# Two layers of a hybrid decoder trunk: moving DMA steps, the write of x and half of the token sums

## Chip, cores and metric

One core of a Trainium2 chip runs the kernel. The metric is device time in microseconds (us), the median of the runs. TensorE (PE) multiplies, VectorE (DVE) and ScalarE (ACT) work on vectors, GpSimd (POOL) on small operations; ACT, POOL and SyncE (SP) issue DMAs, each in the order of its own queue.

## The reference

The kernel computes two decoder layers over 512 tokens of width 1024, all in float32. Each layer adds three things to x:

```
h = rmsnorm(x); x += (gated sum of convolution, sparse attention, latent attention) @ w_out
x += cross_attention(rmsnorm(x), rmsnorm(mem))
gate, up = split(rmsnorm(x) @ w_gate_up);  x += (silu(gate) * up) @ w_down      # hidden width 2816
```

After the second layer comes one more rmsnorm.

## The kernel before

**Products.** A float32 product is made of three matmuls: each operand is cast to a high part (ACT, line 92) and a low part is the difference (DVE, line 93), and high x high, high x low and low x high are summed. Weights go through `raw` (two buffers of 1 MB, loaded by SP, line 101), then `wh` and `wl` (three buffers each). Lines 85 to 87 are one such triple of matmuls (`mm3`); lines 1261 to 1263 are the triple of the last residual.

**Fewer products.** The gate-up product and the down product use a scheme with seven products in place of eight of a 2 x 2 block product, which needs sums and differences of blocks on both sides.
- Weight sums: `summed(l)` lists 152 DMAs ("steps") that copy and add blocks of `w_gate_up` and `w_down` into the DRAM tensors `up` and `down`. They are issued by POOL (line 372, `tick`): every triple of matmuls adds `paced["rate"]` to an account, and when it reaches 1 the next step is issued, tied by a semaphore to that triple. The rate is 0.17 in the mixer and up to the feed-forward part, 0.07 in it. Steps of layer 1 are listed before layer 0's last residual, and there the rate is 0.06. All steps of a layer must be issued before its last residual.
- Token sums: lines 1488 to 1504 make four sums `t` of the normed, transposed x for each half `kk` of the rows (DVE, lines 1494 to 1497, in tiles of the tag `P`, which has 6 buffers) and cast each into `rh` and `rl` (16 tiles of the tag `op`). Both halves are written down ahead of the first gate products, with a low priority (`tc.cur_priority += 100000`): the framework orders every engine's instructions by priority and by when they can run in its own model of the machine.

**Feed-forward part.** First come four blocks of 128 columns in the plain way (two of gate, two of up; 48 matmuls each): each takes one of three PSUM banks `mm`; Silu (line 1513) empties the first two, so the fourth block waits for the first Silu. Then ten rounds of seven products follow.

**Last residual** (`down_residual`). Seven products, one after another (`parts`), of 11 blocks for two token tiles each: 154 triples. `done` adds each into the x tiles, 128 x 512 each, eight in all (`op`, 36 buffers). In layer 0, `after(t)` then issues from ACT the writes of x[t] to the DRAM tensor `xd` (line 1602), two of 256 KB for each token tile. x[t] is complete for two tiles after the fifth product and for the others after the seventh; one half of the first two already after the second.

**Next layer's mixer** (`mix`). It takes the x tiles from SBUF, squares them (ACT, line 209), sums, raises to the power -0.5 (POOL, line 200), multiplies (DVE, line 213), turns the result (PE, line 221) and casts it into `hTh`/`hTl`. A first product over token tiles follows (lines 297 to 299), whose results are cast into the tiles V, and then the blocks of the convolution. After the mixer x is read back from `xd` (line 1184). After the cross-attention, POOL writes x to `xd` once more (line 1420).

Of the kernel before, what the change touches and what calls it, by code (L numbers as in the profile page):

```python
# [12 lines left out]
AF = mybir.ActivationFunctionType  # L13
OP = mybir.AluOpType
# [6 lines left out]
NT = T // 128  # L21
# [30 lines left out]
def kernel(ctx, tc, x, mem, positions, rel_bias, norm_mix, norm_xattn, norm_mem, norm_ffn, norm_final,  # L52
# [5 lines left out]
    nc = tc.nc  # L58
# [14 lines left out]
    def new(tag, shape=(128, 512), dt=F32, name=None):  # L73
        return (odd if tag in ODD else sb).tile(list(shape), dt, name=name or tag, tag=tag, bufs=BUFS[tag])

    def bank(tag, name=None):
        return ps.tile([128, 512], F32, name=name or f"ps_{tag}", tag=tag, bufs=PBUFS[tag])

    def f(ap):
        return ap.bitcast(F32)  # L80
# [8 lines left out]
    def hilo(hi, lo, src, scale=None):  # L89

        if scale is None:
            nc.scalar.copy(hi, src)  # L92
            nc.vector.tensor_tensor(lo, src, f(hi), op=OP.subtract)  # L93
        else:
            nc.scalar.activation(hi, src, AF.Copy, scale=scale)
            nc.vector.scalar_tensor_tensor(lo, src, scale, f(hi), op0=OP.mult, op1=OP.subtract)
# [19 lines left out]
    def fm_blocks(w, cols, kt):  # L116

        per = 2048 // (kt * 128)
        for i in range(0, len(cols), per):
            c = cols[i:i + per]  # L120
            n = len(c)

            def parts(raw):
                rv = raw[:, :kt * n * 128].rearrange("p (k c) -> p k c", k=kt)
                j = 0
                while j < n:
                    e = j + 1
                    while e < n and c[e] == c[e - 1] + 128:
                        e += 1
                    yield (rv[:, :, j * 128:e * 128],  # L130
                           w[:, c[j]:c[j] + (e - j) * 128].rearrange("(k p) c -> p k c", p=128))
                    j = e
            raw = load(parts)
            rv = raw[:, :kt * n * 128].rearrange("p (k c) -> p k c", k=kt)
            for j in range(n):
                yield unit(rv[:, :, j * 128:(j + 1) * 128], (kt, 128))
# [13 lines left out]
    def fm_gemm(*args):  # L150
        run(fm_steps(*args))


    mhalf = low.tile([128, 8], F32, name="mhalf")
# [21 lines left out]
    xd = dr.tile([T, D], F32, name="xd")  # L176
# [11 lines left out]
    def load_gain(vec):  # L188
        g = new("gB", (128, D))
        nc.scalar.dma_start(g, rows_bcast(vec, D))  # L190
        return g

    def rstd_of(ss, n):

        r = new("st", (128, 8), name="rs")
        if n == 2:
            nc.vector.scalar_tensor_tensor(r[:, 0:1], ss[:, 0:1], EPS, ss[:, 1:2], op0=OP.add, op1=OP.add)
        else:
            nc.vector.tensor_scalar(r[:, 0:1], ss[:, 0:1], EPS, None, op0=OP.add)
        nc.gpsimd.tensor_tensor(r[:, 1:2], r[:, 0:1], mhalf[:, 0:1], op=OP.pow)  # L200
        return r[:, 1:2]

    def norm_rows(halves, g):
# [20 lines left out]
    def norm_to_hT(halves, g, t, keep=None):  # L224
        for i, h in enumerate(norm_rows(halves, g)):
            tp = turn(h, 4).rearrange("p (k c) -> p k c", k=4)
            if keep is not None:
                for dst, k in keep[i]:
                    nc.scalar.copy(dst[:, :, t * 128:(t + 1) * 128], tp[:, k:k + dst.shape[1], :])
            hilo(hTh[:, 4 * i:4 * i + 4, t * 128:(t + 1) * 128], hTl[:, 4 * i:4 * i + 4, t * 128:(t + 1) * 128], tp)  # L230

    def show(name, ap, view=None):
        if dbg is not None and name in dbg:
            dst = dbg[name] if view is None else view(dbg[name])
            nc.sync.dma_start(dst, ap)
# [127 lines left out]
    latest = {}  # L363
    paced = {"due": 0.0, "rate": 0.0, "issued": 0, "steps": iter(())}
# [9 lines left out]
                tc.add_manual_dep(d.ins, product.ins.name, mybir.DependencyInfo(  # L374
                    mybir.DependencyClass.Sync, mybir.DependencyReason.DATA), reason="paced")

    def mix(l, x_src, g_mix, x_now, more_x):
        W = w_in[l]


# [31 lines left out]
        for t in range(NT):  # L412
            norm_to_hT(x_now(t), g_mix, t)
            if t == 0:

                with tc.issue_after(latest["normed"].ins):
                    first += islice(units, 2)
        show(f"hT{l}", f(hTh))
        tv = bank("t")
        nc.tensor.transpose(tv[:, 0:124], v1[0:124, 0:128], ident[0:124, 0:124])  # L420
# [66 lines left out]
        for t in range(NT):  # L487
            c = slice(t * 64, (t + 1) * 64)
# [12 lines left out]
        for i, wu in enumerate(fm_blocks(W, [Z_CQ, Z_CQ + 128, Z_CQ + 256, Z_CKV, Z_CKV + 128], KD)):  # L501
            p = bank("mm")
# [323 lines left out]
        fin = []  # L826
# [234 lines left out]
        for t in range(NT):  # L1061
            p = bank(next(idle))
            s = slice(t * 128, (t + 1) * 128)
# [115 lines left out]
    def load_x(src, xs, tiles=range(NT)):  # L1179
        for t in tiles:  # L1180
            hs = []
            for c in range(2):
                h = new("op", name="x")
                nc.sync.dma_start(h, src[t * 128:(t + 1) * 128, c * 512:(c + 1) * 512])
                hs.append(h)
            xs.append(hs)
        return xs

    def down_residual(W, sums, kept, xs, more_x, after):
# [63 lines left out]
        for i, (w, ahead) in enumerate(parts):  # L1253
# [36 lines left out]
            else:  # L1290
                side = then

    xin = x[0]
    x_src = xin
    g_mix = load_gain(norm_mix[0])
    xs = load_x(xin, [], (0,))
    sums, down_sums, paced["steps"] = summed(0)
    for l in range(L):
        fin = mix(l, x_src, g_mix, lambda t: xs[t], lambda: l or load_x(xin, xs, (1, 2, 3)))
        xs = load_x(x_src, [])  # L1300


# [23 lines left out]
        for h, wu in enumerate(fm_blocks(w_xkv[l], [128 * h for h in range(4)], KD)):  # L1326
            p = bank("mm")
# [3 lines left out]
            c = slice((h % 2) * 256, (h % 2 + 1) * 256)  # L1331
# [63 lines left out]
        for k0 in range(0, KD, 4):  # L1395
# [3 lines left out]
            for k1 in range(0, 4, 2):  # L1399
                wh, wl = unit(rv[:, k1:k1 + 2, :], (2, 512))  # L1400
                for k2 in range(2):
                    k = k0 + k1 + k2
                    a, b = mx(k)
                    for t in range(2):
                        s = slice(t * 128, (t + 1) * 128)
# [60 lines left out]
        def keep_act(m, a, b, sign=1.0):  # L1466

            d = act_slot(m)
            for i in range(2):
                q = slice(i * 256, (i + 1) * 256)  # L1470
                nc.vector.scalar_tensor_tensor(d[i], a[:, q], sign, b[:, q], op0=OP.mult, op1=OP.mult)
            hilo(d[2], d[3], d[0])
            if m % 4 == 3 or m == FFN // 128 - 1:

                (b11, b12), (b21, b22) = (h[0:2] for h in kept[-1])
                tc.cur_priority += 100000
                nc.vector.tensor_tensor(b11, b11, b12, op=OP.subtract)
                nc.vector.tensor_tensor(b21, b22, b21, op=OP.subtract)
                nc.vector.tensor_tensor(b21, b21, b11, op=OP.add)
                nc.vector.tensor_tensor(b12, b22, b12, op=OP.subtract)  # L1480
                tc.cur_priority -= 100000
# [3 lines left out]

        q0, q1 = slice(0, 256), slice(256, 512)
        rT = [[None] * 4 for _ in range(4)]
        tc.cur_priority += 100000
        for kk in range(2):
            k2 = slice(2 * kk, 2 * kk + 2)  # L1490
            r11, r12 = hlow[:, k2, q0], hlow[:, k2, q1]
            r21, r22 = hhigh[kk][:, :, q0], hhigh[kk][:, :, q1]
            t = [new("P", (128, 2, 256), name="t") for _ in range(4)]
            nc.vector.tensor_tensor(t[0], r11, r12, op=OP.subtract)
            nc.vector.tensor_tensor(t[2], r22, r12, op=OP.subtract)
            nc.vector.scalar_tensor_tensor(t[1], t[0], -1.0, r22, op0=OP.mult, op1=OP.subtract)
            nc.vector.scalar_tensor_tensor(t[3], t[1], -1.0, r21, op0=OP.mult, op1=OP.subtract)
            for i in range(4):
                h, lo = new("op", (128, 2, 256), F32R, name="rh"), new("op", (128, 2, 256), F32R, name="rl")
                hilo(h, lo, t[i])  # L1500
                for k in range(2):
                    rT[i][2 * kk + k] = h[:, k, :], lo[:, k, :]
        tc.cur_priority -= 100000

        cols = [0, 128, FFN, FFN + 128]
        pg = {}
        for i, wu in enumerate(fm_blocks(w_gate_up[l], cols, KD)):
            m = i % 2
            p = bank("mm")
            fm_gemm(p, wu, hx, KD, ((0, 256), (256, 512)))  # L1510
            if i < 2:
                s = new("P", name="sg")
                nc.scalar.activation(s, p, AF.Silu)  # L1513
                pg[m] = s
            else:
                keep_act(m, pg[m], p)

# [34 lines left out]
        for m in range(2, FFN // 128, 2):  # L1552
            c = m * 128
# [41 lines left out]
        assert not list(paced["steps"])  # L1595
        if not last:
            sums, next_down, paced["steps"] = summed(1)
            paced["issued"], paced["rate"] = 0, 0.06

            def after(t):  # L1600
                for c in range(2):
                    nc.scalar.dma_start(xd[t * 128:(t + 1) * 128, c * 512:(c + 1) * 512], xs[t][c])
        else:
            def after(t):
                for c, h in enumerate(norm_rows(xs[t], g_next)):
                    nc.sync.dma_start(out[0, t * 128:(t + 1) * 128, c * 512:(c + 1) * 512], h)
        xs = []
# [3 lines left out]
        x_src = xd  # L1611
        g_mix = g_next
# [53 lines left out]
```

## Time and profile before

| | us |
|---|---|
| median of 3 runs | 1921.27 (1919.84 to 1921.55) |
| the profiled execution | 1921.47 |
| its span, first to last instruction | 1919.3 |
| PE busy | 1885.0 (98%) |
| DVE busy | 1521.8 (79%) |
| ACT busy | 1039.3 (54%) |
| POOL busy | 265.7 (14%) |
| TensorE clock granted, mean | 0.996 of full speed |

How to read it: "busy" is the time in which an engine has an instruction running. In a timeline row the first number is the start (us from the start of the span), the second the duration; brackets hold the idle time of the engine just before and what ended it. `out<-in` names tiles. PEld is PE's weight load.

### The profile page before, as it was taken

Reading aid. Unit: us, or ns where it says so; the run is one execution under the profiler, and the core shown is the slowest. Engines: PE = TensorE matmul, PEld = TensorE weight load, DVE = VectorE, ACT = ScalarE, POOL = GpSimd, SP = SyncE. Lnnn points to the kernel's source line nnn. Section 1 sums busy time; section 2 is a strip of 40 time slices with the busy share of each in tenths; the row PEclk is TensorE's granted clock in tenths of the full one; section 3 lists DMA queues with packets and bytes.
Section 4 is the critical chain, followed back from the end, with each engine's and each line's share of the span. In section 5 each row is a group of like instructions: output and inputs, shape, how many; then the busy total and the mean of one; then the engine's idle time right before and its main releaser. Section 6 shows DMA issues by size and latency. Waiting matters only on the chain.

```text
span 1919.3 us, 29411 instructions
## 1 busy us (share of the span) xinstructions
PE 1885.0 (98%) x11004; PEld 1647.3 (86%) x11004; DVE 1521.8 (79%) x2797; ACT 1039.3 (54%) x1962; POOL 265.7 (14%) x428
## 2 busy tenths in 40 slices
PE   9999999999999999999999999999999999999998
PEld 8888888888887999998788878888888879999986
DVE  6989899765466899987769999986644678999886
ACT  5366557763255554545544755676633455444564
POOL 1211111111122111000011111111111231100000
PEclk9999999999999999999999999999999999999999
DMA  6666545456776667657756665444566765754654
GB/s 182 152 165 166 160 122 131 121 146 167 212 191 158 176 166 191 168 186 225 224 144 168 162 179 148 123 102 118 160 177 182 216 159 154 197 153 132 198 194 162
DMA packets 213754, 318.49 MB, mean 166 GB/s; under 512 B 15296, under 2 KB 152771, under 8 KB 211564
## 3 DMA queue, kind: packets, MB, share of 16 engines
q1 hardware_dynamic: 179436, 217.16, 35.2%
q0 software_dynamic: 31232, 92.30, 23.6%
q10 hardware_dynamic: 2944, 7.17, 1.1%
q8 instruction: 86, 1.41, 0.3%
q14 instruction: 56, 0.46, 0.1%
HBM read 308.17 MB, written 96.49 MB: 211 GB/s over the span
## 4 chain that ended last, share of the span: by engine, by line
PE 81%; DVE 8%; DMA 3%; issue 3%; ACT 3%; POOL 1%; SPq 0%; POOLq 0%; DVEq 0%; ACTq 0%
PE ps_mm L85 14%; PE ps_mm L86 13%; PE ps_mm L87 13%; PE ps_s L85 3%; PE ps_s L87 2%; PE ps_s L86 2%; PE ps_t L85 2%; PE ps_t L86 2%; PE ps_t L87 2%; PE ps_t L977 2%; DVE wl L93 2%; DMA raw<-down 1%; PE ps_t L221 1%; PE ps_pv L85 1%; DMA raw<-in_w_in_dram 1%
## 5 line engine op out<-in xcount | busy, mean ns | idle before, releaser
L92 ACT CAST wh<-raw 128x1024 fp32r<-128x1024 f32 (+3 forms) x422 | 424.2, 1009 | 493.8 <-PE ps_mm L86 111.5
L93 DVE TENSOR_TENSOR wl<-raw,wh 128x1024 fp32r<-128x1024 f32 (+3 forms) x422 | 490.9, 1170 | 221.4 <-ACT wh L92 220.4
L85 PE MATMUL ps_mm<-hTh,wh 128*128 128x512 f32 (+1 forms) x1152 | 415.4, 361 | 3.0 <-ACT sg L1513 2.5
L86 PE MATMUL ps_mm<-hTl,wh 128*128 128x512 f32 (+1 forms) x1152 | 412.4, 358 | 0.0
L87 PE MATMUL ps_mm<-hTh,wl 128*128 128x512 f32 (+1 forms) x1152 | 411.9, 358 | 0.4 <-DVE wl L93 0.4
L87 PEld LDWEIGHTS ps_mm<-hTh,wl 128*128 128x128 f32 x1152 | 218.3, 190 | 32.8 <-DVE wl L93 1.2
L85 PEld LDWEIGHTS ps_mm<-hTh,wh 128*128 128x128 f32 x1152 | 218.4, 190 | 32.4 <-ACT sg L1513 2.9
L86 PEld LDWEIGHTS ps_mm<-hTl,wh 128*128 128x128 f32 x1152 | 218.5, 190 | 26.7 <-issue 0.7
L480 DVE SCALAR_TENSOR_TENSOR ca<-u,vT,ca 128x512 f32<-128x512 f32 x240 | 177.3, 746 | 2.9
L372 POOL DMA_DIRECT2D up<-in_w_gate_up_dram x128 | 84.9, 664 | 579.4 <-PE ps_mm L87 385.4
L372 POOL DMA_DIRECT2D down<-in_w_down_dram x132 | 85.0, 644 | 470.0 <-PE ps_mm L87 256.6
L92 ACT CAST PTh<-ps_t 128x512 fp32r<-128x512 f32 (+4 forms) x136 | 70.4, 518 | 60.7 <-PE ps_t L977 46.8
L940 ACT ACTIVATE P<-P,ss 128x512 f32<-128x512 f32 (+3 forms) x128 | 71.3, 558 | 49.8 <-DVE ss L937 48.9
L85 PE MATMUL ps_s<-rh,wh 128*128 128x256 f32 x320 | 90.6, 283 | 0.0
L86 PE MATMUL ps_s<-rl,wh 128*128 128x256 f32 x320 | 90.6, 283 | 0.0
L87 PE MATMUL ps_s<-rh,wl 128*128 128x256 f32 x320 | 90.6, 283 | 0.0
L93 DVE TENSOR_TENSOR PTl<-ps_t,PTh 128x512 fp32r<-128x512 f32 (+2 forms) x120 | 71.5, 597 | 9.1 <-ACT PTh L92 8.0
L948 ACT ACTIVATE P<-P,sr 128x512 f32<-128x512 f32 (+3 forms) x128 | 63.2, 554 | 17.3 <-DVE sr L946 17.1
L85 PE MATMUL ps_mm<-op,wh 128*128 128x512 f32 (+1 forms) x192 | 68.7, 358 | 0.0
L86 PE MATMUL ps_mm<-op,wh 128*128 128x512 f32 (+1 forms) x192 | 68.2, 355 | 0.0
L87 PE MATMUL ps_mm<-op,wl 128*128 128x512 f32 (+1 forms) x192 | 68.2, 355 | 0.0
L85 PEld LDWEIGHTS ps_s<-rh,wh 128*128 128x128 f32 x320 | 61.4, 192 | 0.0
(539 smaller groups left out, 4660.5 us busy)
## 6 DMA issues: line engine op xcount, KB each, us to landing
up<-in_w_gate_up_dram POOLq DMA_DIRECT2D x128, 320.0 KB, 4.5
down<-in_w_down_dram POOLq DMA_DIRECT2D x132, 256.0 KB, 4.1
raw<-in_w_in_dram SPq DMA_DIRECT2D x32, 1024.0 KB
raw<-in_w_gate_up_dram SPq DMA_DIRECT2D x60, 512.0 KB
raw<-up SPq DMA_DIRECT2D x40, 512.0 KB
raw<-down SPq DMA_DIRECT2D x16, 1024.0 KB
raw<-in_w_in_dram SPq DMA_DIRECT2D x26, 512.0 KB
raw<-in_w_down_dram SPq DMA_DIRECT2D x12, 1024.0 KB
```

What stands on the lines that cost most here:

```text
L85: nc.tensor.matmul(o, lh, rh, start=start, stop=False)
L86: nc.tensor.matmul(o, lh, rl, start=False, stop=False)
L87: tick(nc.tensor.matmul(o, ll, rh, start=False, stop=stop))
L92: nc.scalar.copy(hi, src)
L93: nc.vector.tensor_tensor(lo, src, f(hi), op=OP.subtract)
L221: nc.tensor.transpose(tp[:, c * 128:(c + 1) * 128], src[:, c * 128:(c + 1) * 128], ident)
L372: d = nc.gpsimd.dma_start(dst, src, accum_op=op) if op else nc.gpsimd.dma_start(dst, src)
L480: nc.vector.scalar_tensor_tensor(c, u[:, j:j + T], cw[:, m, j:j + 1], c, op0=OP.mult, op1=OP.add)
L940: nc.scalar.activation(p[:, c], p[:, c], AF.Exp, bias=s[:, k:k + 1], scale=-1.0, accum_out=s[:, 4 + k:5 + k])
L948: nc.scalar.activation(P[k], P[k], AF.Copy, scale=r[:, k:k + 1])
L977: nc.tensor.transpose(tp[:, w:w + 128], P[k][:, j * 128:(j + 1) * 128], ident)
```

## The change

Three edits. (1) Layer 0's last residual issues no steps: the rate is 0 there. (2) ACT no longer writes x to `xd` in that residual; POOL does, in layer 1's mixer, ordered on its queue behind the last power of the four norms. (3) In both layers the second half of the token sums is written down after the first Silu, and its instructions on ACT are ordered behind that Silu.

```diff
-        nc.gpsimd.tensor_tensor(r[:, 1:2], r[:, 0:1], mhalf[:, 0:1], op=OP.pow)
+        latest["power"] = nc.gpsimd.tensor_tensor(r[:, 1:2], r[:, 0:1], mhalf[:, 0:1], op=OP.pow)
...
-    def mix(l, x_src, g_mix, x_now, more_x):
+    def mix(l, x_src, g_mix, x_now, more_x, spill_x):
...
+        if l:
+            with tc.issue_after(latest["power"].ins):
+                spill_x()
         show(f"hT{l}", f(hTh))
...
+    def spill(xs):
+        for t in range(NT):
+            for c in range(2):
+                nc.gpsimd.dma_start(xd[t * 128:(t + 1) * 128, c * 512:(c + 1) * 512], xs[t][c])
...
-        tc.cur_priority += 100000
-        for kk in range(2):
+        def token_sums(kk):
...
+            tc.cur_priority += 100000
             nc.vector.tensor_tensor(t[0], r11, r12, op=OP.subtract)
...
-        tc.cur_priority -= 100000
+            tc.cur_priority -= 100000
+        token_sums(0)
...
-                nc.scalar.activation(s, p, AF.Silu)
+                act_ins = nc.scalar.activation(s, p, AF.Silu)
                 pg[m] = s
+                if i == 0:
+                    with tc.issue_after(act_ins.ins):
+                        token_sums(1)
...
-            paced["issued"], paced["rate"] = 0, 0.06
+            paced["issued"], paced["rate"] = 0, 0.0
             def after(t):
-                for c in range(2):
-                    nc.scalar.dma_start(xd[t * 128:(t + 1) * 128, c * 512:(c + 1) * 512], xs[t][c])
+                pass
```

`tc.issue_after(ins)` orders the instructions made in its block behind `ins` on the engine of `ins`, without a semaphore.

## Rows read from the trace of the kernel before

**Rows 1.** The page's busy times: share of the span and instructions of each engine.

```profile
PE 1885.0 (98%) x11004; PEld 1647.3 (86%) x11004; DVE 1521.8 (79%) x2797; ACT 1039.3 (54%) x1962; POOL 265.7 (14%) x428
```

**Rows 2.** Busy time in four stretches: both last residuals, norms, layer 1's gate products.

```profile
core 0: us, PE busy (x) PEld busy (x) DVE busy (x) ACT busy (x) POOL busy (x), PEclk, DMA share, GB/s
853.20:964.90 111.70, 107.19 (x466) 86.54 (x466) 84.60 (x117) 59.53 (x88) 9.06 (x18) 1.00 0.71 219
1804.70:1909.70 105.00, 105.00 (x464) 86.44 (x463) 84.98 (x119) 59.41 (x88) 3.48 (x3) 1.00 0.56 186
965.00:986.00 21.00, 19.81 (x129) 18.18 (x128) 16.04 (x44) 12.40 (x34) 1.67 (x2) 1.00 0.43 127
...
1600.00:1804.70 204.70, 204.70 (x1708) 204.70 (x1707) 181.90 (x249) 98.65 (x148) 14.22 (x20) 1.00 0.58 164
```

**Rows 3.** Waits of PE over the run: us in total, times, longest us.

```profile
PE ps_t L221 <- DVE hn L213: 3.0, 5, 1.4
PE ps_mm L85 <- ACT sg L1513: 2.5, 2, 1.2
...
PE ps_mm L1262 <- DVE wl L93: 1.5, 2, 0.8
PE ps_mm L1261 <- ACT wh L92: 1.4, 1, 1.4
PE ps_t L1262 <- DVE wl L93: 1.3, 2, 0.8
```

**Rows 4.** Chain that ended last, in layer 0's last residual: start, us, what.

```profile
950.25 6.86 DMA raw<-down
```

**Rows 5.** Timeline of POOL in layer 0's last residual: the steps.

```profile
948.06 0.84 POOL L372 DMA_DIRECT2D up<-in_w_gate_up_dram  x1 [8.52 <-PE ps_mm L1263]
962.66 0.53 POOL L372 DMA_DIRECT2D up<-in_w_gate_up_dram  x1 [13.76 <-PE ps_mm L1263]
```

**Rows 6.** Instructions on `xd`: duration in ns, least, median, most; first and last start.

```profile
L1420 POOL DMA_DIRECT2D xd<-x x16: 539/584/915, 614.8 to 1577.5; - x16
L1602 ACTq DMA_DIRECT2D xd<-x x8: 326/327/444, 885.1 to 965.8; - x8
...
DMA to landing us min/median/max: 2.4/4.7/5.9
```

**Rows 7.** Timeline of ACT in layer 0's last residual.

```profile
949.19 1.06 ACT L92 CAST wh<-raw 128x1024 fp32r<-128x1024 f32 x1 [2.39 <-DVE x L1218]
```

**Rows 8.** Timeline of POOL in five places.

```profile
626.05 0.58 POOL L1420 DMA_DIRECT2D xd<-x  x1
...
935.68 0.56 POOL L200 TENSOR_TENSOR rs<-rs,mhalf 128x1 f32<-128x1 f32 x1 [6.05 <-DVE rs L197]
...
970.71 1.11 POOL L200 TENSOR_TENSOR rs<-rs,mhalf 128x1 f32<-128x1 f32 x1 [2.80 <-DVE rs L197]
989.96 0.57 POOL L372 DMA_DIRECT2D up<-in_w_gate_up_dram  x1 [18.15 <-PE ps_mm L87]
...
1702.81 0.81 POOL L372 DMA_DIRECT2D down<-down  x1 [6.22 <-PE ps_mm L87]
```

**Rows 9.** Timeline of SP in layer 1's mixer: a load of weights.

```profile
979.50 0.37 SPq L101 DMA_DIRECT2D raw<-in_w_in_dram  x1
```

**Rows 10.** Timeline of DVE: norms, and a weight difference in layer 0's gate blocks.

```profile
626.14 1.42 DVE L213 SCALAR_TENSOR_TENSOR hn<-x,rs,gB 128x512 f32<-128x512 f32 x2
...
641.37 1.22 DVE L93 TENSOR_TENSOR wl<-raw,wh 128x1024 fp32r<-128x1024 f32 x1
...
936.28 1.42 DVE L213 SCALAR_TENSOR_TENSOR hn<-x,rs,gB 128x512 f32<-128x512 f32 x2 [0.68 <-POOL rs L200]
```

**Rows 11.** Timeline of ACT around layer 0's first Silu.

```profile
643.23 0.62 ACT L92 CAST rh<-t 128x512 fp32r<-128x512 f32 x1 [1.57 <-DVE t L1496]
643.86 1.28 ACT L1513 ACT_TABLE_LOAD   x1
```

**Rows 12.** Timeline of PE: the fourth gate block's first matmul.

```profile
645.81 0.39 PE L85 MATMUL ps_mm<-hTh,wh 128*128 128x256 f32 x1 [1.24 <-ACT sg L1513]
```

**Rows 13.** Timeline of ACT in layer 1's mixer: the first cast of V.

```profile
980.70 0.21 ACT L92 CAST op<-ps_mm 128x64 fp32r<-128x64 f32 x1
```

More of the change, by code (lines that the diff above doesn't have):

```diff
@@ L1298 @@
     for l in range(L):
-        fin = mix(l, x_src, g_mix, lambda t: xs[t], lambda: l or load_x(xin, xs, (1, 2, 3)))
+        fin = mix(l, x_src, g_mix, lambda t: xs[t], lambda: l or load_x(xin, xs, (1, 2, 3)), lambda: spill(xs))
         xs = load_x(x_src, [])
```

## The prediction, made before the change was run

> **What bounds the kernel now.** I read the busy shares first: TensorE (PE) is busy for 1885.0 of 1919.3 us [rows 1]. So only the remaining stops of PE can be won, and each is worth no more than its own length. The profiled execution took 1921.47 us for that span, 2.17 us lying around it; it stands 0.2 us over the median of the runs, 1921.27 us.
>
> Next I read the stretches that the edits touch [rows 2]. Both layers end in the same residual, seven products of PE, and the reader should compare the two: layer 0's lasts 111.7 us with PE busy for 107.19, layer 1's lasts 105.0 us with PE busy throughout. In layer 0 the DMA share is 0.71, in layer 1 0.56. Layer 1's has no paced DMA step and writes nothing to `xd`. It is a control for this change within the same trace.
>
> Then the waits of PE [rows 3]: the three rows on lines 1261 and 1262 (1.5, 1.4, 1.3 us) can come from that residual alone, since layer 1's has no stop; with a small one of 0.3 us that is not shown they make the 4.5 us by which PE falls short of 111.7. All wait for a cast weight, `wh` or `wl`. The chain through the residual says why the weights are late [rows 4]: 6.86 us pass at the last load of `down`, which at six blocks of 128 x 512 is the smallest, 768 KB.
>
> **Part 1: no DMA steps in layer 0's last residual.** The pace falls from 0.06 to 0. The residual has 7 x 11 x 2 = 154 ticks, so 154 x 0.06 = 9 steps leave it; rows 5 show the eighth and the last of the nine, each reading and writing 320 KB (64 rows of 1280 numbers). They sit beside the loads that PE waits for: the step at 948.06 is in flight when the last load is issued at 950.25 [rows 4, 5].
>
> **Part 2: x goes to DRAM later, from GpSimd.** Eight writes of 256 KB leave ScalarE's queue, issued from 885.1 to 965.8, amid the loads of weights [rows 6]. They cost twice: in DMA time, and in ScalarE's order. At 949.19 a cast had waited 2.39 us for VectorE's sums of `x` [rows 7], which the write issue ahead of it in the queue needed and the cast didn't; the last load waits for the buffer behind such casts.
>
> I cost parts 1 and 2 together, since each stop has both beside it. The upper bound is the whole difference of the residuals, 111.7 - 105.0 = 6.7 us; the lower one is PE's missing busy time, 4.5 us, and the difference between them is slower matmuls around each stop. Layer 0 also turns two tiles of the next norm in that time (about 0.3 us of transposes), so I take 6.4 us. What is late next: the first weights of layer 1's mixer, which share the end of this residual; their casts wait for PE there, not for the load, so I expect no new stop.
>
> **Where the eight writes go.** They are ordered behind the last power of the next norms, which ran from 970.71 to 971.82 [rows 8]. GpSimd's next work was a step at 989.96, so the queue is free for 18.1 us; eight issues take 8 x 0.584 = 4.7 us, or 7.3 us at the longest of 0.915 [rows 6, 8]. No wait is added for `x`: the last norm has read it by then. Behind the issues stand only steps. On the DMA queues they add 2 MB to a stretch (965 to 986) whose share is 0.43 [rows 2]. One landing takes 4.7 us; overlapped, all end near 971.8 + 4.7 + 5.9 = 982 to 985, one after another near 971.8 + 8 x 4.7 = 1009. The weight load issued at 979.50 [rows 9] meets them. PE starts on it only after two more blocks, 48 matmuls at 105.0/464 = 0.23 us [rows 2], so 11 us after 986; at the slow 6.86 us of rows 4 it lands at 986.4, a cast and a difference take 1.06 and 1.22 [rows 7, 10], and it can come 8 us late for nothing. I cost the writes at 0. The lower end is 0 too, as nothing on PE's path leaves this stretch; the upper is 4.7 us, the whole length of the issues, as if they stopped the norm beside them.
>
> Rows say of the issues' effect on VectorE: an issue of `xd` began at 626.05, and the norm's two multiplications that began at 626.14 took 1.42 us, as the two at 936.28 without an issue beside them [rows 8, 10]. The power at 970.71 took 1.11 us against 0.56 at 935.68 [rows 8]: GpSimd does wait for VectorE. The Trainium skill (SBUF — State Buffer, Who interferes with whom) says that VectorE and GpSimd share one port pair, that one holds it for a whole instruction and that the other blocks; by that rule, taken at its hardest, eight issues in the norm would stop VectorE for their whole length. By that rule the sum would be 4.7 us worse; the trace agrees for the power and not for the issues. I go by the rows.
>
> **Where the nine steps go.** Layer 1 issues every step nine places later. Its last step is now at 1702.81 [rows 8]; nine more at a pace of 0.07 are 129 ticks of three matmuls, and 1708 matmuls in 204.7 us are 0.12 us each [rows 2], so 46 us: the last comes near 1749, before the next residual at 1804.7. PE is busy 204.70 of 204.70 us there with steps in the first half, so they cost 0. Between, the number of steps per time stays, but a step's turn meets other work: the longest stop on a norm's `hn` is 1.4 us [rows 3], and one such may go or come. I take 0, with 1.5 us to either side.
>
> **Part 3: the first Silu ahead of half of the sums.** In both layers the fourth block of the gate product waits for the bank that the first Silu empties: 2.5 us of idle PE in two stops [rows 3]. In layer 0, ScalarE casts an `rh` of the second half at 643.23, loads a table for 1.28 us from 643.86 and only then runs Silu [rows 11]; PE resumes at 645.81 after 1.24 us idle [rows 12]. The matmul after the stop takes 0.39 us where the pitch is 0.12 [rows 2], so I add 0.15 us a stop for the lost overlap: 2.5 + 0.3 = 2.8 us. Silu's input was ready far earlier: the block is finished two blocks before. With four `rh` casts moved behind it, and their `t` tiles no longer holding the slots that Silu's output needs, its table load can start before 641, and 1.95 us after that start (643.86 to 645.81) PE could go on. The next to be late is the fourth block's `wl`, done by 641.37 + 1.22 = 642.59 at the latest [rows 10], ahead of 645.81 - 1.24 = 644.57. The moved casts must be done before the first product with `rh`, 48 + 24 matmuls or 8.6 us later. Bounds: 0 if ScalarE's order is unchanged, and 3.0 with 0.25 us a stop.
>
> **Sum.** 6.4 + 2.8 = 9.2 us: 1921.47 - 9.2 = 1912.27 for an execution like the profiled one, 1912.1 against the median; I say 1912.2.
>
> **Rivals.**
> *The debt is paid elsewhere.* Steps and writes cost 6.4 us wherever they land, because loads of weights run all the time. For it: the DMA share is 0.43 or more in every stretch of rows 2. Against: the steps in layer 1's gate products cost PE nothing, and 965 to 986 is the emptiest of those stretches. Then only Silu is won: 1921.3 - 2.8 = 1918.5. Chance 0.09.
> *The third edit does not do what it says*: ScalarE runs the first Silu no earlier, and only the residual is won: 1921.3 - 6.4 = 1914.9. Chance 0.08.
> *VectorE is blocked by the eight issues*: 1912.2 + 4.7 = 1916.9. The power's 1.11 us [rows 8] shows that the two engines can hold each other up, rows 10 show no hold in this direction. Chance 0.05. The Trainium skill's rule on the port pair, above, would bring this case about.
> *Slower: the late writes hold x's eight slots.* `op` has 36 slots; until the writes land, eight are taken. Early in the mixer the casts of V need four, from 980.70 on [rows 13], and V's banks hold up the next products. If these casts are given slots of `x`, PE stops until the writes have landed: at worst 1009 - 980.7 = 28.7 us, which gives 1912.2 + 28.7 = 1940.9. It turns the sign once the landing comes later than 980.7 + 9.2 = 990. Against: after the residual all other 28 slots are empty. Chance 0.04.
>
> **How the numbers follow.** The forecast has 0.74: 1912.2, from 1921.3 - 6.7 - 3.0 - 1.5 = 1910.1 to 1921.3 - 4.5 - 2.5 + 1.5 = 1915.8. The range 1909.8 to 1917.3 adds the second and third rivals and 0.3 below, and leaves out the debt and the slower case, and some of the forecast's own tails. A measurement of this kernel can tell some 0.2%, 3.8 us: faster is below 1917.4. Faster gets 0.74 + 0.08 + 0.05 less 0.02 for tails, 0.85; the same 0.11; slower 0.04.
>
> **What would show it.** Right: layer 0's last residual lasts 105 to 106 us with PE busy throughout; no wait of PE on Silu's `sg`; eight issues of `xd` by GpSimd between the fourth power and the first step, and layer 1's last step near 1740 (1749 less the gain). Wrong: PE waiting on lines 1261 and 1262 as before (then the loads were late for another reason), a stop at V's casts or in the norms at 965 (slots or ports), or Silu still behind `rh`. Above all the prediction fails if the stops of layer 0 come back in layer 1's mixer.

## The result and the profile after

The changed kernel takes 1910.09 us (median of 6 runs, 1907.94 to 1912.27); the kernel before, beside it, 1921.38. The ratio is 0.994 with a 95% interval of 0.9927 to 0.9952, which is 9.2 to 14.0 us won. The forecast was 1912.2, in a range of 1909.8 to 1917.3: right in sign, inside the range 0.3 us above its lower end, and 2.1 us short in its middle. The profiled execution took 1907.94 us, of which 1906.2 us are the span.

The busy times of the page of the kernel after answer to [rows 1]: PE is still the bound, with 7.4 us less of busy time, since matmuls around a stop (0.39 us in [rows 12] for a pitch of 0.12), and at half clock, count as busy for longer.

```profile
PE 1877.6 (98%) x11004; PEld 1643.4 (86%) x11004; DVE 1522.5 (80%) x2797; ACT 1038.8 (54%) x1962; POOL 269.1 (14%) x436
```

Busy times by stretch of the kernel after, columns as in [rows 2]: layer 0's last residual and layer 1's.

```profile
850.30:955.00 104.70, 104.70 (x465) 86.58 (x464) 85.48 (x118) 60.15 (x89) 3.11 (x9) 1.00 0.58 191
1791.00:1896.00 105.00, 105.00 (x464) 86.40 (x462) 85.78 (x119) 59.27 (x88) 3.47 (x3) 1.00 0.56 187
```

Layer 0's residual now looks like its control: PE without a stop, and a DMA share of 0.58 for 0.71. Measured from the start of the same first matmul to the start of the same first matmul behind it, it fell from 111.65 to 105.08 us; this length is used for every kernel below. Each is read from one profiled execution; layer 1's residual, which no edit touches, takes 104.8 to 106.0 us (first matmul to last) over the profiles of this document, so a difference of less than about 1 us between two of them says nothing.

The stage behind it didn't come out as foreseen. These are its first 100 or so matmuls, in the kernel before and then in the kernel after, between the starts of the same two matmuls.

```profile
964.92:981.67 16.75, 15.56 (x102) 13.93 (x100) 13.19 (x26) 9.67 (x21) 1.67 (x2) 1.00 0.39 108
```

```profile
955.43:972.62 17.19, 15.19 (x101) 14.01 (x100) 13.10 (x25) 9.16 (x19) 6.01 (x10) 1.00 0.62 198
```

It takes 0.44 us more, and PE idles more in it: 17.19 - 15.19 = 2.00 us for 1.19. Where, the waits of PE of the kernel after tell, to be held against [rows 3] (us in total, times, longest us).

```profile
PE ps_t L221 <- DVE hTl L93: 3.1, 4, 1.4
PE ps_t L221 <- DVE hn L213: 2.9, 6, 0.8
```

The rows on the residual's weights are gone, and so is the one on Silu's `sg`. New is a longer wait on `hTl`: in this stage PE stops for 1.44 us over the usual pitch of its matmuls at 957.2, where before there were 0.43 and 0.35. The timelines of ScalarE and of VectorE in the kernel after show what stands ahead of it; the third is VectorE's in the kernel before.

```profile
955.00 1.44 ACT L92 CAST wh<-raw 128x688 fp32r<-128x688 f32 x2
956.34 1.07 ACT L92 CAST hTh<-ps_t 128x512 fp32r<-128x512 f32 x2
```

```profile
956.04 0.75 DVE L213 SCALAR_TENSOR_TENSOR hn<-x,rs,gB 128x512 f32<-128x512 f32 x1 [0.66 <-POOL rs L200]
956.71 0.68 DVE L1221 TENSOR_TENSOR x<-x,ps_mm 128x512 f32<-128x512 f32 x1
957.31 0.87 DVE L93 TENSOR_TENSOR wl<-raw,wh 128x688 fp32r<-128x688 f32 x1
958.09 1.28 DVE L93 TENSOR_TENSOR hTl<-ps_t,hTh 128x512 fp32r<-128x512 f32 x2
```

```profile
965.72 0.87 DVE L93 TENSOR_TENSOR wl<-raw,wh 128x688 fp32r<-128x688 f32 x1
966.51 0.69 DVE L93 TENSOR_TENSOR hTl<-ps_t,hTh 128x512 fp32r<-128x512 f32 x1
...
967.94 0.75 DVE L213 SCALAR_TENSOR_TENSOR hn<-x,rs,gB 128x512 f32<-128x512 f32 x1 [0.68 <-POOL rs L200]
```

ScalarE casts one weight more ahead of `hTh`, but `hTh` is no later for it: it starts 0.91 us after the stage's first matmul, 0.86 before. VectorE is what is late. Its first `hTl` starts 2.66 us after that matmul where it was 1.59, because the next norm's `hn`, for which VectorE also waits 0.66 us on GpSimd's power, now stands in its queue ahead of a sum of x, a weight difference and `hTl`. In the kernel before that `hn` came behind the first `hTl`.

Silu is where it was forecast. This is ScalarE's timeline in the kernel after: the table load begins at 636.99 and the first Silu ends at 638.89, where the load alone began at 643.86 before [rows 11]. The second `sg` of the layer is the row at 642.38.

```profile
636.99 1.28 ACT L1523 ACT_TABLE_LOAD   x1
638.29 0.60 ACT L1523 ACTIVATE sg<-ps_mm 128x512 f32<-128x512 f32 x1
...
642.38 0.60 ACT L1523 ACTIVATE sg<-ps_mm 128x512 f32<-128x512 f32 x1 [1.00 <-DVE rl L93]
```

GpSimd's timeline of the kernel after shows the writes behind the fourth power, as ordered, then nothing until a step at 981.59; the last line is layer 1's last step.

```profile
960.98 1.11 POOL L200 TENSOR_TENSOR rs<-rs,mhalf 128x1 f32<-128x1 f32 x1 [4.97 <-DVE rs L197]
962.05 4.39 POOL L1299 DMA_DIRECT2D xd<-x  x8
981.59 0.52 POOL L372 DMA_DIRECT2D up<-in_w_gate_up_dram  x1 [15.15 <-PE ps_mm L87]
...
1734.96 0.80 POOL L372 DMA_DIRECT2D down<-down  x1 [4.60 <-PE ps_s L87]
```

### The profile page after: what moved, and what is told of

It is laid out like the page before. It is cut to its first block, busy times and chain, and to the rows that moved or that the text cites. A ratio compares the mean times of both kernels' runs of the same rounds, so it can differ in the third digit from the quotient of the medians.

```text
span 1906.2 us, 29430 instructions
## 1 busy us (share of the span) xinstructions
PE 1877.6 (98%) x11004; PEld 1643.4 (86%) x11004; DVE 1522.5 (80%) x2797; ACT 1038.8 (54%) x1962; POOL 269.1 (14%) x436
## 3 DMA queue, kind: packets, MB, share of 16 engines
q8 instruction: 86, 1.41, 0.3%
## 4 chain that ended last, share of the span: by engine, by line
PE 87%; DVE 5%; issue 3%; ACT 2%; DMA 1%; POOL 1%; SPq 0%; POOLq 0%; DVEq 0%; ACTq 0%
PE ps_mm L85 14%; PE ps_mm L87 14%; PE ps_mm L86 14%; PE ps_s L85 3%; PE ps_s L87 3%; PE ps_s L86 3%; PE ps_t L85 2%; PE ps_t L86 2%; PE ps_t L87 2%; PE ps_t L980 2%; PE ps_mm L1265 1%; PE ps_mm L1266 1%; PE ps_mm L1264 1%; PE ps_pv L85 1%; PE ps_pv L87 1%
## 5 line engine op out<-in xcount | busy, mean ns | idle before, releaser
L372 POOL DMA_DIRECT2D down<-down x44 | 36.4, 828 | 179.2 <-PE ps_mm L87 58.6
```

The costliest lines, as they stand in the source:

```text
L372: d = nc.gpsimd.dma_start(dst, src, accum_op=op) if op else nc.gpsimd.dma_start(dst, src)
```

## The experiments

### Which of the two DMA edits ends the residual's stops

**No steps alone** (`e1_no_steps`), the kernel before with one line changed:

```diff
-            paced["issued"], paced["rate"] = 0, 0.06
+            paced["issued"], paced["rate"] = 0, 0.0
```

> The kernel before with the pace of layer 0's last residual set to 0 and nothing else. Theory A (steps and writes each take DMA time from the weight loads, and the writes also hold ScalarE's queue): the middle stop (914 to 920, 2.3 us), which has steps alone beside it, goes; the stops at 898 and 956, which have both, shrink but do not vanish. Residual of layer 0 106.5 to 108.5 us against 111.7, time 1916.5 to 1918.5 us. Rival B (the steps alone do it): residual 105 us, time near 1915. Rival C (only ScalarE's wait behind the write issues does it): residual 111 us, time near 1921.

**Writes moved alone** (`e2_writes_moved`), the kernel before with the second edit, the nine steps staying:

```diff
+        if l:
+            with tc.issue_after(latest["power"].ins):
+                spill_x()
...
             def after(t):
-                for c in range(2):
-                    nc.scalar.dma_start(xd[t * 128:(t + 1) * 128, c * 512:(c + 1) * 512], xs[t][c])
+                pass
```

> The kernel before with the eight writes of x moved to GpSimd behind the norms, the steps staying at 0.06, the token sums as before. Theory A: the middle stop stays, the other two shrink; residual 107 to 109.5 us, time 1916.5 to 1919. Rival B (steps alone): residual 111 to 112 us, time near 1921. Rival C (ScalarE's wait alone): residual 105 us, time near 1915. If the writes cost PE anything in the new place, a stop of 1 to 5 us appears between 965 and 1000 us.

The residual by itself, in the kernel without steps and then in the one with moved writes (columns as in [rows 2]):

```profile
851.90:957.80 105.90, 105.75 (x466) 86.63 (x466) 85.81 (x118) 60.03 (x88) 3.10 (x9) 1.00 0.62 206
```

```profile
851.92:960.10 108.18, 106.15 (x466) 86.54 (x465) 84.72 (x118) 60.23 (x90) 9.04 (x18) 1.00 0.69 210
```

Without steps the residual takes 105.90 us with stops of 0.20 and 0.28 us, though ScalarE still issues eight writes in it; the run takes 1911.62 us, ratio 0.9956 (0.9943 to 0.9968), less than any of the three theories gave. With the writes moved and the steps left it takes 108.20, with stops of 0.81, 0.68 and, at the last `down` load, 0.26 and 1.03 us, as theory A had it; the run takes 1919.09, 0.1 over theory A's band, ratio 0.9989 (0.998 to 0.9998). So taking the steps out suffices, and theory A, by which the stops with writes beside them would only shrink, falls with the first of the two kernels. The writes do make the stops longer, but only while the steps are there.

One load shows how: the last of `down`, which the chain before pointed at [rows 4]. ScalarE's timeline has the first cast from it and, in brackets, how long ScalarE was idle for it. Kernel before, no steps alone, writes moved alone, after:

```profile
957.21 1.57 ACT L92 CAST wh<-raw 128x1024 fp32r<-128x1024 f32 x2 [6.02 <-DMA raw<-down]
```

```profile
949.91 1.61 ACT L92 CAST wh<-raw 128x1024 fp32r<-128x1024 f32 x2 [3.62 <-DMA raw<-down]
```

```profile
952.40 1.57 ACT L92 CAST wh<-raw 128x1024 fp32r<-128x1024 f32 x2 [4.96 <-DMA raw<-down]
```

```profile
947.64 1.76 ACT L92 CAST wh<-raw 128x1024 fp32r<-128x1024 f32 x2 [3.51 <-DMA raw<-down]
```

SyncE issued that load at 950.3, 945.4, 946.6 and 943.3 in these four. From issue to cast it took 6.9 us with steps and writes, 5.8 with steps, 4.5 with writes, 4.3 with neither. The steps cost it 1.5 to 2.4 us, the writes 1.1 beside steps and 0.2 without. Through what the transfers hold each other up, no run shows.

**The amount of steps.** Twice as many (`e9_double_steps`, 18) and half as many (`e12_half_steps`, 4), in the kernel before:

```diff
-            paced["issued"], paced["rate"] = 0, 0.06
+            paced["issued"], paced["rate"] = 0, 0.12
```

> The kernel before with twice as many DMA steps in layer 0's last residual (18 instead of 9; nothing else changed). Theory S, that each step's reading and writing on the DMA engines makes the loads and the writes late: stops grow from 6.6 us to 10 to 14 us, the residual to 115 to 119 us, and the median to 1923.5 to 1928 (layer 1 then has nine steps fewer behind it, which can give up to 2 us back). Rival (the nine steps only tip the stage over, and more of them cost nothing further, since the loads wait for buffers): residual 111 to 113 us, median within 1.5 us of the kernel before.

The half has 0.03 there.

> The kernel before with half of the steps in layer 0's last residual (4 or 5 instead of 9). So far: none 105.9 us, nine 111.65, eighteen 113.6. Theory S by amount (each step adds to the DMA time that the loads share): 108 to 110 us, stops of 2.5 to 4 us in sum. Rival (a stop comes only where a step falls on a load that is due, so few steps can cost as much or nothing): 106 to 107 us or over 110.5 us. Median 1914 to 1919.

The residual with 18 steps, then with 4:

```profile
853.65:967.20 113.55, 109.34 (x466) 87.42 (x466) 84.89 (x117) 58.98 (x88) 15.25 (x27) 0.98 0.79 243
```

```profile
851.40:960.70 109.30, 107.05 (x466) 87.73 (x465) 84.80 (x117) 59.73 (x88) 5.82 (x13) 0.98 0.66 208
```

GpSimd's timeline with 4 steps, all four of them:

```profile
874.36 0.56 POOL L372 DMA_DIRECT2D up<-in_w_gate_up_dram  x1 [8.09 <-PE ps_s L1263]
...
896.80 0.52 POOL L372 DMA_DIRECT2D up<-in_w_gate_up_dram  x1 [8.67 <-PE ps_mm L1263]
...
920.03 0.80 POOL L372 DMA_DIRECT2D up<-in_w_gate_up_dram  x1 [8.03 <-PE ps_t L1263]
...
942.47 0.84 POOL L372 DMA_DIRECT2D up<-in_w_gate_up_dram  x1 [8.66 <-PE ps_mm L1263]
```

With 18 steps the stops are at the places that they have with nine, but for one of 0.55 us more at 932.4, and sum to 5.6 us, not 10 to 14; with nine they sum to 5.8. The stretch is 1.9 us longer, but 3.4 us at half clock lie in it, from 961.6. With 4 steps the three earlier stops are gone and the one at the last `down` load is whole, 1.65 + 1.03 = 2.7 us: one step was issued at 942.47, the load at 944.5, and it took 7.2 us to its cast. No step began between 896.80 and 920.03, where the loads behind the stops of 914 to 919 were issued (901.8 to 914.2 in this kernel). The other three steps met loads too: loads were issued 0.9 to 2.0 us behind each of them, at 876.35, 897.71 and 921.56, and PE didn't stop. So with no steps the stops come to 0.8 us at most (over all of the kernels below), with 4, 9 and 18 to 2.7, 5.8 and 5.6 us: they don't grow by the step. A step makes a stop only beside a load that PE is about to need; how much slack the other loads had was not measured.

With 4 steps the length, 109.28 us with 3.4 us at half clock from 953.5, and the sum of the stops lie in the bands of the amount theory and outside the rival's; it is the places, three stops gone and one whole, that speak for the rival. With 18, the length and the stops lie below the amount theory's bands. The medians are 1918.75 for 4 steps (ratio 0.9988, 0.9977 to 0.9999; the ten times lie in two groups, 1916.1 to 1917.1 and 1920.4 to 1922.6, and the profile is of the first) and 1929.8 for 18 (1.0045, 1.0033 to 1.0057), over both bands: more is lost with 18 than the residual shows, and the part on layer 1 tells where some of it goes.

### Silu, and the kernel after again

**Silu alone** (`e3_silu_only`), the kernel before with the third edit of the change and nothing else.

> The kernel before with the second half of the token sums behind the first Silu in both layers; steps and writes as before. Theory: the two stops of 1.4 us at the fourth gate block go, nothing else moves: 2.8 us less, 1918.6 us; residual of layer 0 stays at 111.7 us. Rival (the order of ScalarE's other work sets the block, Silu is only the last name): stops of 1 us or more stay there under another name, 1920 to 1921.4 us.

The median is 1917.01, ratio 0.9982 (0.9971 to 0.9992); that is 1.6 us under the expected time, and the interval holds the expected gain. Both stops on `sg` are gone. From the matmul ahead to the first of the fourth gate block 1.52 us pass in layer 0 and 1.53 in layer 1 in the kernel before, and 0.12 here and in the kernel after, 2.8 us less in sum. The residual still has stops, 5.0 us in sum, and takes 112.64 us with 3.4 us at half clock in it (from 946.3), so the third edit's gain doesn't hang on the other two.

**The kernel after, a second time** (`e4_after_again`), unchanged.

> The changed kernel once more. Its profiled execution was 13.5 us under the profiled one of before, its median 11.3 us. Theory: the profile of before held two 3.4 us windows at half clock (at 167.0 and 1115.9 us) of 1.6 us each that the first profile of the changed kernel lacked by chance; they come and go between executions, so this median is 1909 to 1912 and some execution shows such a window again (mean clock 0.996 or 0.997). Rival: the change itself keeps the clock up; then every execution has a mean clock of 0.998 and the time is 1908 us.

It has a median of 1909.69, ratio 0.9945 (0.9932 to 0.9957), and a profiled span of 1909.5 us, 3.3 us over the first one's 1906.2, with the residual at 105.62. Most of the difference is TensorE's clock. Three stretches at half clock, near 13, 167 and 1109 us, are in this profile and in that of the kernel before, and not in the first profile of the kernel after. Kernel before, and the place that answers to it in the first profile of the kernel after:

```profile
167.00:170.40 3.40, 3.40 (x11) 2.61 (x10) 3.16 (x9) 2.26 (x6) 0.51 (x1) 0.50 0.28 74
```

```profile
166.00:169.40 3.40, 3.14 (x16) 2.67 (x17) 3.37 (x11) 2.86 (x9) 0.51 (x1) 1.00 0.20 47
```

In the same 3.4 us PE starts 11 matmuls at a granted clock of 0.50 (1.2 GHz) and 16 at 1.00 (2.4 GHz). So some 3 us of the 13.1 us by which the two profiled spans differ are not the change's doing; medians are the measure. The mean clock of the five executions lies between 0.996 and 0.999, which rules out the rival.

### What the moved writes do

**Steps out and Silu early, the writes left on ScalarE** (`e8_no_steps_silu`), the kernel after without its second edit:

```diff
-        if l:
-            with tc.issue_after(latest["power"].ins):
-                spill_x()
...
             def after(t):
-                pass
+                for c in range(2):
+                    nc.scalar.dma_start(xd[t * 128:(t + 1) * 128, c * 512:(c + 1) * 512], xs[t][c])
```

> The kernel after, but with the eight writes of x left on ScalarE inside the residual: steps taken out and first Silu early, without the moved writes. Theory S (the steps alone make the residual's stops; beside that the moved writes are worth nothing and cost about 1 us in the norms by the order that comes with them): residual 105.4 to 106.3 us, norm stage without the 1.4 us stop at hTl, median 1907.5 to 1909.5, no slower than the kernel after. Rival M (the moved writes still carry a part that the steps' removal leaves): one or more stops of 0.5 us or longer in the residual, 106.5 us or longer, and a median 1 to 2.5 us above that of the kernel after (1910.1).

The residual takes 105.11 us and PE is busy throughout:

```profile
850.25:955.35 105.10, 105.10 (x466) 86.78 (x465) 85.36 (x118) 59.95 (x88) 3.11 (x9) 1.00 0.64 207
```

The median is 1908.79, ratio 0.9936 (0.9924 to 0.9948); the kernel after has 1910.09 and 1909.69, and the intervals overlap. As far as medians can tell, two of the three edits give all that is won; theory S holds, with a residual 0.3 us under its band, and rival M's residual and median don't come. The norms have their old stops of 0.83, 0.42 and 0.33 us and the old order: VectorE's first `hTl`, at 956.97, is ahead of the next norm's `hn`, at 958.39, and ScalarE has one weight cast ahead of the `hTh` casts and a write's issue between them:

```profile
954.95 0.77 ACT L92 CAST wh<-raw 128x688 fp32r<-128x688 f32 x1
...
956.25 0.56 ACT L92 CAST hTh<-ps_t 128x512 fp32r<-128x512 f32 x1
956.30 0.33 ACTq L1613 DMA_DIRECT2D xd<-x  x1
```

**The writes in the residual, but from GpSimd** (`e5_writes_pool_residual`), as the last diff with `nc.gpsimd` for `nc.scalar`.

> The kernel after, but with the eight writes of x in the residual as before, issued by GpSimd instead of ScalarE, and no steps there. It tells the writes' transfer time from ScalarE's issuing, and what brings the new order of casts in the norms. If that order comes because ScalarE no longer issues the writes, the norm stage has the stops of the kernel after (about 0.9 and 1.4 us near 955 to 962); if it comes with the writes being put into the norms, the stage runs as in the kernel without steps (0.8, 0.4 and 0.3 us). Theory S: residual 105.1 to 106.0 us either way, median within 1.5 us of the kernel after. Rival (writes in flight delay the loads of the residual whoever issues them): 106.5 us or longer and 1 to 3 us slower than the kernel after.

**The writes without an order behind the last power** (`e6_unordered`):

```diff
-            with tc.issue_after(latest["power"].ins):
-                spill_x()
+            spill_x()
```

> The kernel after without the order behind the last power: GpSimd may issue the eight writes of x between the norms' powers. If the writes' descriptors hold VectorE off, or a late power holds up the norms, stops on hn or hTl of 1 to 4 us are added in the 10 us behind the residual and the median is 1911 to 1914; if the place of the writes on GpSimd is free, as the kernel after's trace suggests (eight issues in 4.39 us with no matmul late by them), it is within 0.5 us of the kernel after.

In both GpSimd issues the eight writes at nearly the same times, 881.6 to 958.8 and 880.7 to 958.2: without the order they move back into the residual by themselves, and only the last is issued between the last two powers. So that kernel doesn't test what eight issues among the powers would do; that stays open. The residual takes 105.85 and 105.75 us, inside theory S's band, the ratios are 0.9946 (0.9933 to 0.9959) and 0.9944 (0.9932 to 0.9956), as the kernel after. And both have the new stops, 0.89 and 1.45 us. That settles where the new order in the norms comes from: every kernel in which ScalarE no longer issues the writes has it (writes moved alone 0.89 and 1.45, after 0.89 and 1.44), wherever they go, and no other has. The stage's first 100 or so matmuls take 16.6 to 16.8 us in the seven profiles with the writes on ScalarE, 17.2 to 17.3 in four of those without, and 18.7 in these two, in which the clock falls (last section). It is the leaving that brings the order; why it comes out so, no run shows.

### The steps in layer 1

With 18 steps, PE stood for 4.03 us over its pitch at 1570.5, in layer 1's cross-attention residual, waiting for a norm's `hn`. At that matmul it is 1.58 in the kernel before and 0.2 in every kernel without steps in layer 0's residual. The kernel after has a stop of 0.95 at a later norm instead, at 1565.2, as have its second profile and the two kernels whose writes GpSimd issues in the residual; with the writes kept on ScalarE there is none. GpSimd's timeline with 18 steps:

```profile
1564.13 0.82 POOL L372 DMA_DIRECT2D down<-down  x1
1567.07 1.16 POOL L1420 DMA_DIRECT2D xd<-x  x2 [2.12 <-DVE x L1176]
1572.41 0.88 POOL L372 DMA_DIRECT2D down<-down  x1 [4.17 <-DMA down<-down]
1572.99 0.89 POOL L200 TENSOR_TENSOR rs<-rs,mhalf 128x1 f32<-128x1 f32 x1
```

The step at 1572.41 waited 4.17 us for the step before it to land, and the norm's power stands behind it in GpSimd's queue. If so, the number of steps that fell out of layer 0's residual decides which step meets which norm. To test that a step makes such a stop, **no steps in layer 1's cross-attention residual**, on the kernel after (`e10_no_steps_cross`) and on the one with the writes kept (`e11_no_steps_both`):

```diff
+        if l:
+            paced["rate"] = 0.0
         residual(lambda k: ox[k], 4, w_xo[l], xs, lambda t: norm_to_hT(xs[t], g_f, t, keep))
```

> The kernel after, with no DMA steps in layer 1's cross-attention residual either (its steps come later, in layer 1's MLP). Theory Q (a step that waits in GpSimd's queue holds the norms' power behind it: stops at hn near 1566 us of 1.58 us in the kernel before, 0.95 in after, none in the kernel with the writes kept, 4.03 with double steps): no stop at hn between 1540 and 1580 us, 0.8 to 1.2 us won there, median 1908.5 to 1909.5. Rival (VectorE or the x writes make hn late): the stop of about 0.95 us stays and the median is that of after (1909.7 to 1910.1). If the steps put off into the MLP make its loads late, the median is 1910.5 or more.

> The kernel without steps in layer 0's last residual and with the early first Silu, the writes of x kept on ScalarE, and no DMA steps in layer 1's cross-attention residual. Theory Q: since that kernel showed no stop at hn there, nothing is won: span within 1 us of 1907.0, median 1907.5 to 1909.3; with the kept writes the norms' stops are 0.8, 0.4 and 0.3 us. Rival (steps in the MLP make loads late): stops at wl or wh between 1610 and 1780 us and a median over 1910.

The waits of PE between 1540 and 1620 us in the first of them, a complete answer:

```profile
PE ps_t L221 <- DVE hTl L93: 0.2, 1, 0.2
```

The stop on `hn` is gone in the first, the second has none, as the kernel that it was made from, and no stop came in the MLP: theory Q holds. In the time it can't be seen: 1909.59 (ratio 0.9937, 0.9925 to 0.995) and 1909.6 (0.9932, 0.9918 to 0.9945), 0.1 and 0.3 us over the bands that I gave and inside the spread of single executions (1908.31 to 1911.7, 1906.21 to 1909.98). The second also had a stop of 0.82 us in the residual (106.03 us). None of the kernels of this part can be told from the kernel after by its median.

## Why the prediction was right, point by point

**Parts 1 and 2, 6.4 us.** The residual gained 111.65 - 105.08 = 6.6 us. The size came from the control, layer 1's residual, and held. The attribution didn't: I costed the edits together "since each stop has both beside it", which is a row read as a cause. Without steps alone the residual is at 105.90 and 105.11 us (with Silu early), so of the 6.6 us the steps take 5.8 to 6.5. The writes moved alone shorten the residual by 3.4 us, and by nothing that can be read once the steps are out. The last load is of three blocks of 128 x 512, not of six; its 768 KB are right, and nothing hangs on the number of blocks.

**ScalarE's order.** I read the cast at 949.19, 2.39 us idle [rows 7], as held up by a write's issue ahead of it. That is misread. The timeline has the two writes' issues behind the cast:

```profile
949.22 0.81 ACTq L1602 DMA_DIRECT2D xd<-x  x2
```

The cast also waits for its own load, issued at 944.13, whose data were in at 949.09 by the trace, when VectorE's sum ended too. So it could hardly have started sooner, whatever stood in ScalarE's queue. The kernel with the steps out still issues its writes from ScalarE and has no stop over 0.28 us. The sum did not suffer from this wrong step, since its size came from the control; that is luck.

**The writes in their new place, 0.** The issues took 4.39 us for eight, 0.55 each, inside the gap counted on (to 981.59), and nothing of x's slots was late. What I missed stands under "I expect no new stop": I looked for what the writes meet where they go, not for what their leaving does to the order of the next stage. The sign that I named, "a stop ... in the norms at 965", came, but neither slots nor ports made it: it is there with the writes issued in the residual too. It cost 0.44 us at the first norms.

**VectorE and the issues.** VectorE's timeline of the kernel after: one `hn` multiplication ahead of the eight issues, a weight difference beside the fourth power, and two multiplications beside the issues (962.05 to 966.44).

```profile
959.29 0.74 DVE L213 SCALAR_TENSOR_TENSOR hn<-x,rs,gB 128x512 f32<-128x512 f32 x1
...
960.82 0.87 DVE L93 TENSOR_TENSOR wl<-raw,wh 128x688 fp32r<-128x688 f32 x1
...
962.81 1.41 DVE L213 SCALAR_TENSOR_TENSOR hn<-x,rs,gB 128x512 f32<-128x512 f32 x2
```

The two beside the issues take 1.41 us, as the two at 936.28 with none beside them [rows 10], so the rival at 1916.9 is out. The Trainium skill (SBUF — State Buffer, Who interferes with whom) says of the port pair that VectorE and GpSimd share that one holds it for a whole instruction while the other blocks. By that rule the power's 1.11 us at 960.98, twice the usual, is such a block, by the difference that runs from 960.82 to 961.69, and the trace agrees there. The same section of the Trainium skill limits the rule, for a VectorE instruction with two inputs in SBUF, to GpSimd instructions that read SBUF. The eight issues held up no such instruction here, so the prediction took the rule too hard.

**The nine steps, 0 with 1.5 to either side.** They gave something. The stop at 1129.5 for a cast of the compression's weights (1.04 us over the pitch, and 0.27 at the matmul behind it) is in every kernel with nine or four steps in layer 0's residual and in none without; with 18 it is not there, but one of 1.25 us stands earlier, at 1093.4. The stop on `hn` of 1.58 us at 1568 went, and the one of 0.95 came. One of 1.3 near 1270 became one of 0.6 at 1258.7; that one is not surely the steps' doing, as other kernels without steps have 0.5 to 1.1 there. Together that is 1.31 + 0.63 + 0.67 = 2.6 us, against which a new stop of 0.6 us at 1527.5, in layer 1's cross-attention, is in this profile. So about 2 us net, most of what the forecast fell short by. The term was mis-sized, just over its own bound; its mechanism, that "a step's turn meets other work" and a stop on `hn` may go, was right. The last step came at 1734.96, where "near 1740" stood.

**Part 3, 2.8 us.** Measured 1.40 + 1.41 = 2.8 us.

**The sum.** 6.6 + 2.8 + 2.0 - 0.4 = 11.0 us; the medians differ by 1921.38 - 1910.09 = 11.3. That they agree so well is in part luck: the terms are read from one profile of each kernel, stops of half a microsecond come and go between executions (the one at 1527.5 is not in the second profile of the kernel after), and the interval of the gain is 9.2 to 14.0 us. For the kernel without steps alone the same terms are 5.75 in the residual, 1.31 at the compression's cast and 1.36 at `hn`, 8.4 us for a measured 9.5. The rival of the debt paid elsewhere (1918.5) is out: the loads of layer 1's mixer, beside writes and steps, made no stop near 10 us, and its DMA share there of 0.62 did no harm.

## What to carry over

When two transfers run beside a late load, take each out alone before dividing the gain: here one of them, the paced steps, was nearly the whole cause, and twice as many made no longer stops: what mattered was whether one ran beside a load that was about to be needed. Work paced by a count meets different neighbours after any change upstream, and where it shares a queue with something short and urgent (a norm's power behind a step that waits for another's landing) a stop can come or go far from the edit. And taking instructions off one engine can change the order that a scheduler gives the next stage, on other engines too (here VectorE's), so look at that order as well as at the load.

## What the runs showed that was not expected

TensorE's granted clock falls to 0.50 for about 3.4 us shortly behind stops of PE, in some executions and not in others. Apart from one at the end of each run, all these places have two stops, or one long one, just ahead. In the kernels with the writes from GpSimd in the residual and without the order it fell at 960.3 and 960.4, behind the stops of 0.89 and 1.45 us in the norms; this is the first of them.

```profile
960.30:963.70 3.40, 3.40 (x16) 3.28 (x15) 2.99 (x6) 1.18 (x2) 1.13 (x1) 0.50 0.97 252
```

In the kernel after, twice, in the one with the writes moved alone and in the one without steps in the cross-attention, the same two stops were followed by no fall. With 18 steps it fell at 1576.0, behind the stop of 4.03 us, so that a stop can cost more than its length. What decides between executions wasn't found out.
